# A gate vector's product moved from the attention of the first token half to the early feed-forward

## Chip, cores and metric

The kernel runs on one core of a Trainium2 chip. The metric is the device time of one execution in microseconds (us). The engines are TensorE (PE, with its weight loads shown as PEld), VectorE (DVE), ScalarE (ACT), GpSimd (POOL) and SyncE (SP, which here only issues transfers). They work side by side, each through its own list of instructions in a fixed order, and wait for each other by semaphores.

## What is computed

One layer of a decoder trunk for 1024 tokens of width 1024, in float32: a modulation by a conditioning vector, three mixers, an output projection, a feed-forward of width 4096. Cut to what matters here:

```
mod = silu(c) @ w_ada + b_ada
sh1, sc1, ga1, sh2, sc2, ga2 = split(mod, 6)          # vectors of 1024; their index v is 0..5
h = rms_norm(x, norm1_g) * (1 + sc1) + sh1
proj = h @ w_in
o_a = sliding window attention;  o_b = S5 state space;  o_c = sparse attention
mix = concat(rms_norm(o_a), rms_norm(o_b), rms_norm(o_c))
x = x + ga1 * (mix @ w_out)
h = rms_norm(x, norm2_g) * (1 + sc2) + sh2
x = x + ga2 * (square(relu(h @ w_ff1)) @ w_ff2)
```

The vector that the change concerns is ga2 (v = 5), the gate of the feed-forward. It is first needed when the feed-forward of the first token half is complete.

## The kernel before

Tokens are worked in eight tiles of 128 (n = 0 to 7), in two halves. The stages follow each other: modulation and first norm; input projection and S5; attention A and then C for tiles 0 to 3 (with their output projection, residual and second norm beside it); attention of tiles 4 to 7 mixed with the feed-forward of the first half; output projection of the second half; feed-forward of the second half, in which TensorE does almost nothing but 128x512 products. Each float32 product is made of three: every operand is split in a high part (a copy on ACT) and a low part (a subtraction on DVE or POOL).

The feed-forward of the first half can't begin before tile 3 has gone through all of its steps: the last attention unit, `finish_steps` (square, scaling by the norm's gain on POOL, high part on ACT, low part on DVE), the projection with `WO`, `residual`, and `norm2_steps`.

**A gate vector.** Each of the six vectors is made from eight slabs of `w_ada` (128 x 1024 float32, 512 KB each, one for each 128 outputs j). Vectors 2 to 5 are made by `ada2`, slab by slab: a transfer on SP's queue, eight ACT instructions that scale 128 columns each with one element of silu(c) (`prod` with `on_act`), a sum over 1024 columns on DVE, a product with a column of ones on PE, whose one column of output is evacuated by a small DVE addition. At the end of vectors 2 and 5 one transposition on PE, a copy on DVE and a transfer of 4 KB put the vector into `mod_d`, from where `load_row(5)` fetches it as a row for all partitions. The lines:

```
def ada2(v, pace):
    for j in range(KD):
        slab = page(1024)
        nc.sync.dma_start(out=slab, in_=I["ada"][v, j])
        yield pace
        a, z = page(128, "s"), tbank()[:, 0:1]
        prod(a, slab, True)
        PE.matmul(out=z, lhsT=a, rhs=ones[:, 0:1], start=True, stop=True)
```

**What sets the order.** Nothing is written out by hand. Steps are recorded in the order of a plan: each has a plan time, and generators such as `ada2` say after how much plan time their next step comes. `F_ADA` gives for each vector the plan time of its first slab and the pace between its steps. The recorded calls are then ordered by `arrange`: for each engine it takes the ready instruction that was recorded earliest, with fixed prices for each kind of instruction, PSUM banks and buffers. Plan times are numbers of that planner and no times of the chip.

**Buffers.** `page(1024)` takes one of 38 buffers with the tag b (4 KB in each partition). Slabs, their products, raw weights, and their high and low parts all share these; a transfer waits on SP until its buffer is free, and everything behind it on SP's queue waits too. PSUM: the small product of a slab takes its turn in the banks that the transpositions use (`tbank`), three during the attention of the first half, two beside the feed-forward.

Of the kernel before, what the change touches and what calls it, by code (L numbers as in the profile page):

```python
# [33 lines left out]
LAG = 2  # L34
BACC = dict(dynamic_dma_scratch_size=1024)
MOD_N = 2
F_ADA = {2: (40.0, 3.0), 4: (64.0, 5.0), 3: (110.0, 5.0), 5: (240.0, 5.0)}
F_LOAD, F_ROT, A_START = 0.635, 3.5, 0.0
A_DUR, A_LEAD, A_GAP = 6.0, 8.0, 2.0
P_START, P_TILE, C_START, C_CMP, C_LEAD0, C_CPACE = 2.38, 7.0, 0.0, 27.6, 5.0, 2.0  # L40
# [270 lines left out]
def trunk(ctx: ExitStack, tc: tile.TileContext, I, out):  # L311
# [85 lines left out]
    def spawn(t, gen, after=None):  # L397
        put(t, (gen, after))
# [924 lines left out]
# [9 lines that stand above are left out]
            b = VT[:, 16 + v * 8 + j:17 + v * 8 + j]  # L1332
            if v == 4:
                stt(mod_c[v][:, j:j + 1], z, 1.0, b, ALU.add, ALU.add)
            else:
                tt(mod_c[v][:, j:j + 1], z, b, ALU.add)
        if v == 4:
            tt(mod_c[v], mod_c[v], VT[:, 8:16], ALU.mult)
        if v in (2, 5):
            z, r = tbank()[0:8, 0:128], page(128)[0:8]  # L1340
            PE.transpose(z, mod_c[v], ident)
            V.tensor_copy(out=r, in_=z)
            nc.scalar.dma_start(out=mod_d[v // 3], in_=r)
        done.add(f"mod {v}")
# [5 lines left out]
    def front():  # L1350
        for v, (t0, pace) in F_ADA.items():
            spawn(t0, ada2(v, pace))
        spawn(now[0] + 40, load_group("aq", 2.0))
        yield from startup()
        t0 = now[0]
        spawn(t0, s5_taps(), "parameters")
        spawn(t0 + 0.5, paced(s5(), S_PACE), "parameters")
        spawn(t0 + F_ROT, paced(s5_rotation_table(), R_PACE))
        spawn(t0 + F_CA, s5_readout_table(), "rotation")
        names = NAMES  # L1360
        width = dict(WGROUPS)
        groups = dict(akv=group_akv, aq=group_aq, cq=group_cq, cmp=group_cmp, ck=group_ck, cv=group_cv)
        for i, name in enumerate(names):
            if name == A_AT:
                spawn(now[0], a_phase(), "KA")
                slow[0] = A_SLOW
            if i + 1 < len(names):
                dur = width[name] * 24 * 8 / 2400.0 * slow[0]
                spawn(now[0] + F_LOAD * dur, load_group(names[i + 1], dur * 0.1))
            yield from groups[name]()  # L1370
            if name == "cmp":
                spawn(now[0] + C_CMP, paced(compresses(), C_CPACE), "s5 taken")
        spawn(now[0] + P_START, early_ab())
        spawn(now[0], c_phase(), "compressed 1")
# [890 lines left out]
```

## Time and profile before

| what | value |
|---|---|
| three runs | 1403.05, 1407.94 and 3282.17 us; median 1407.94 us |
| profiled execution | 1406.35 us |
| its span, from the first to the last instruction | 1404.6 us |
| outside of the span | 1.75 us |
| TensorE's clock granted over the span, share of full | 0.962 |
| busy: PE, DVE, ACT, POOL | 1330.2, 973.0, 796.8, 652.9 us |

The page and the answers count an engine as busy while an instruction of it runs; matmuls are pipelined and their ends are modelled, so that a busy PE may still have slack. In a list of instructions in order of time, the bracket behind a row is the idle time of the engine just before it, and who ended it. Most program lines carry one line number (2201, where the recorded calls are played), so rows are told apart by tile names: b, u, s, q, k and r are buffer tags, pa and pb PSUM banks, small a collection of columns. Every slab product on ACT reads `b<-b,small 128x128`.

### The profile page before, as it was taken

What the parts mean: (1) busy time and instruction counts of PE and PEld (TensorE: products, weight loads), DVE (VectorE), ACT (ScalarE), POOL (GpSimd) and SP (SyncE); (2) the same over time, 40 slices, a digit from 0 to 9 for tenths busy, and PEclk for the clock granted to TensorE, in tenths of its full rate; (3) what the DMA queues carried; (4) which work ended last, traced back from release to release, by engine and by line L of the source; (5) the groups of instructions that cost most, each with busy time, mean ns of one, the idle gap of its engine ahead of it and who ended that gap; (6) DMA issues with size and microseconds to landing.
All of it is one profiled execution on the core that took longest, in us unless ns stands there. A gap on an engine that the chain in (4) does not pass through costs nothing.

```text
span 1404.6 us, 20524 instructions
## 1 busy us (share of the span) xinstructions
PE 1330.2 (95%) x7134; PEld 1142.1 (81%) x7134; DVE 973.0 (69%) x2005; ACT 796.8 (57%) x1816; POOL 652.9 (46%) x640
## 2 busy tenths in 40 slices
PE   5799799999899868999999999999999999999998
PEld 4689799999898647888888888888887888888886
DVE  7867658788688764556565566564559787888796
ACT  5368457777679766655556565553253545444450
POOL 2646756413656544546545546575564221222231
PEclk9979899999899877999999999999999999999999
DMA  9434434523224231222222232233556423233231
GB/s 360 151 106 134 153 101 135 196 81 106 66 73 147 94 134 37 96 68 72 75 68 88 75 98 68 99 111 109 168 175 241 164 77 102 94 107 118 64 102 60
DMA packets 59429, 160.55 MB, mean 114 GB/s; under 512 B 6431, under 2 KB 22333, under 8 KB 59325
## 3 DMA queue, kind: packets, MB, share of 16 engines
q1 hardware_dynamic: 51517, 145.33, 31.0%
q10 hardware_dynamic: 7808, 13.91, 2.7%
q8 instruction: 56, 0.92, 0.3%
q14 instruction: 48, 0.39, 0.1%
HBM read 140.07 MB, written 19.14 MB: 113 GB/s over the span
## 4 chain that ended last, share of the span: by engine, by line
PE 72%; DVE 5%; ACT 4%; issue 1%; DMA 0%; POOL 0%; ACTq 0%
PE pb L2201 41%; PE pa L2201 31%; ACT b L2201 3%; DVE b L2201 2%; ACT u L2201 1%; DVE pb L2201 1%; DVE k L2201 0%; DVE u L2201 0%; DMA cq_d<-s 0%; DVE small L2201 0%; DVE s L2201 0%; ACT s L2201 0%; ACT k L2201 0%; POOL s L2201 0%; ACTq L2201 0%
## 5 line engine op out<-in xcount | busy, mean ns | idle before, releaser
L2201 PE MATMUL pb<-b,b 128*128 128x512 f32 (+2 forms) x2478 | 591.9, 386 | 3.7 <-DVE b L2201 3.7
L2201 PEld LDWEIGHTS pb<-b,b 128*128 128x128 f32 (+1 forms) x2478 | 446.9, 190 | 87.3 <-DVE b L2201 5.1
L2201 POOL TENSOR_TENSOR b<-b,b 128x1024 fp32r<-128x1024 f32 (+6 forms) x140 | 317.7, 2276 | 319.2 <-ACT b L2201 211.5
L2201 PE MATMUL pa<-b,b 128*128 128x256 f32 (+2 forms) x1974 | 367.3, 336 | 10.8 <-DVE b L2201 6.0
L2201 PEld LDWEIGHTS pa<-b,b 128*128 128x128 f32 (+1 forms) x1974 | 302.4, 195 | 44.5 <-DVE b L2201 8.0
L2201 ACT ACTIVATE b<-b 128x1024 fp32r<-128x1024 f32 (+5 forms) x265 | 241.1, 926 | 114.1 <-DVE b L2201 44.4
L2201 DVE TENSOR_TENSOR b<-b,b 128x1024 fp32r<-128x1024 f32 (+4 forms) x181 | 203.2, 1153 | 18.2 <-ACT b L2201 11.2
L2201 PE MATMUL pa<-u,b 128*128 128x384 f32 (+2 forms) x836 | 208.1, 369 | 4.4 <-ACT u L2201 2.4
L2201 PEld LDWEIGHTS pa<-u,b 128*128 128x128 f32 x836 | 148.9, 208 | 15.6 <-ACT u L2201 7.9
L2201 DVE TENSOR_TENSOR b<-pa,b 128x512 f32<-128x512 f32 (+3 forms) x176 | 108.6, 626 | 69.7 <-PE pa L2201 66.1
L2201 ACT ACTIVATE u<-pa 128x384 fp32r<-128x384 f32 (+4 forms) x205 | 97.2, 479 | 93.5 <-PE pa L2201 91.0
L2201 DVE TENSOR_TENSOR u<-pa,u 128x384 fp32r<-128x384 f32 (+1 forms) x173 | 95.0, 553 | 63.0 <-ACT u L2201 59.9
L2201 DVE TENSOR_TENSOR b<-pb,b 128x512 f32<-128x512 f32 (+2 forms) x120 | 76.0, 647 | 53.0 <-PE pb L2201 51.0
L2201 POOL TENSOR_SCALAR b<-b,small 128x64 f32<-128x64 f32 (+8 forms) x118 | 78.1, 673 | 61.7 <-DVE small L2201 51.7
L2201 POOL TENSOR_SCALAR u<-u,small 128x256 f32<-128x256 f32 (+3 forms) x90 | 52.6, 595 | 115.2 <-DVE small L2201 78.7
L2201 PE MATMUL pa<-wide,b 128*128 128x128 f32 (+1 forms) x443 | 84.4, 303 | 14.5 <-DVE b L2201 10.2
L2201 ACT ACTIVATE b<-b,small 128x128 f32<-128x128 f32 x256 | 93.3, 529 | 1.8 <-DMA b<-in_ada_dram 0.9
L2201 PEld LDWEIGHTS pa<-wide,b 128*128 128x128 f32 (+1 forms) x443 | 59.4, 152 | 33.7 <-DVE b L2201 13.0
L2201 PE MATMUL pb<-k,u 128*128 128x320 f32 (+10 forms) x300 | 73.0, 352 | 8.6 <-ACT u L2201 5.8
L2201 ACT ACTIVATE b<-pb,small 128x64 f32<-128x64 f32 (+4 forms) x130 | 62.2, 493 | 30.1 <-DVE small L2201 24.5
L2201 POOL TENSOR_TENSOR b<-r,b 128x512 fp32r<-128x512 f32 x37 | 52.3, 1412 | 54.8 <-ACT b L2201 54.6
L2201 ACT ACTIVATE u<-pb,small 128x256 f32<-128x256 f32 (+6 forms) x126 | 59.7, 484 | 28.3 <-DVE small L2201 26.4
(150 smaller groups left out, 1511.1 us busy)
## 6 DMA issues: line engine op xcount, KB each, us to landing
b<-in_ff_dram SPq DMA_DIRECT2D x128, 512.0 KB, 3.9
b<-in_ada_dram SPq DMA_DIRECT2D x48, 512.0 KB, 5.2
b<-in_x_dram SPq DMA_DIRECT2D x16, 512.0 KB, 6.1
b<-in_wo_dram SPq DMA_DIRECT2D x16, 512.0 KB, 4.5
r<-in_w_in_dram SPq DMA_DIRECT2D x16, 256.0 KB, 2.7
b<-in_cw_dram SPq DMA_DIRECT2D x8, 512.0 KB, 4.5
x_d<-b ACTq DMA_DIRECT2D x8, 512.0 KB, 4.1
out_dram<-b SPq DMA_DIRECT2D x16, 256.0 KB, 3.0
```

The lines of the kernel that those rows point to most:

```text
L2201: method(*args, **kw)
```

## The change

One entry of the table changes. The first slab of vector 5 gets plan time 560 in place of 240, and the pace between its steps is 8 in place of 5.

```
-F_ADA = {2: (40.0, 3.0), 4: (64.0, 5.0), 3: (110.0, 5.0), 5: (240.0, 5.0)}
+F_ADA = {2: (40.0, 3.0), 4: (64.0, 5.0), 3: (110.0, 5.0), 5: (560.0, 8.0)}
```

What is computed stays the same. The order of all engines changes from the attention of the first half on, because `arrange` orders anew around the gap and around the new place.

**First place, ACT, the end of tile 3's attention.** Here s_717 (before) and s_707 (after) are the attention output of tile 3, s_769 and s_750 its squares, b_768 and b_749 its high part; b_773, b_779 are products of the last two slabs; small is fed by exponentials of tile 4's first unit (u_775, u_753). Before:

```order
L2201 ACTIVATE b_773<-b_766,small 128x128 x4
L2201 ACTIVATE b_779<-b_774,small 128x128 x2
L2201 ACTIVATE s_767<-pa_66 64x384
L2201 ACTIVATE small<-small 128x1
L2201 ACTIVATE u_770<-pa_65,small 128x384
L2201 ACTIVATE u_775,small<-pb_67,small 128x256 x2
L2201 ACTIVATE u_775,small<-pb_68,small 128x256
L2201 ACTIVATE s_769<-s_717 128x384
L2201 ACTIVATE small<-small 128x1 x2
L2201 ACTIVATE b_779<-b_774,small 128x128 x3
L2201 ACTIVATE b_768<-s_717 128x384
L2201 ACTIVATE b_779<-b_774,small 128x128 x3
```

And now, where b_766 is the high part of a feed-forward weight:

```order
L2201 ACTIVATE b_766<-b_765 128x1024
L2201 ACTIVATE s_748<-pa_66 64x384
L2201 ACTIVATE small<-small 128x1 x2
L2201 ACTIVATE u_753,small<-pb_67,small 128x256
L2201 ACTIVATE u_751<-pa_65,small 128x384
L2201 ACTIVATE s_750<-s_707 128x384
L2201 ACTIVATE u_753,small<-pb_67,small 128x256
L2201 ACTIVATE u_753,small<-pb_68,small 128x256
L2201 ACTIVATE small<-small 128x1
L2201 ACTIVATE b_749<-s_707 128x384
```

The slab products are gone from between the steps of tile 3, and a copy of a feed-forward weight has moved ahead of them.

**Second place, DVE and POOL, a few steps on.** On DVE, before, the sum of the last slab (s_778) stands between the masks of tile 4 (ISA) and the low part of tile 3 (b_768):

```order
L2201 ISA pb_67,small<-pb_67,u_465,small 128x256
L2201 ISA small 128x1
L2201 TENSOR_REDUCE s_778<-b_779 128x128
L2201 TENSOR_TENSOR b_768<-s_717,b_768 128x384
L2201 TENSOR_REDUCE small<-small 128x3
```

Now:

```order
L2201 ISA pb_67,small<-pb_67,u_465,small 128x256
L2201 ISA small 128x1
L2201 TENSOR_TENSOR b_749<-s_707,b_749 128x384
L2201 TENSOR_REDUCE small<-small 128x3
L2201 RECIPROCAL small<-small 128x3
```

On POOL, before, with b_789 the low part of the first feed-forward weight and s_717 as above:

```order
L2201 TENSOR_TENSOR s_717<-s_717,small 128x384
L2201 TENSOR_SCALAR u_775<-u_775,small 128x256
L2201 TENSOR_SCALAR small<-small 128x1
L2201 TENSOR_SCALAR u_775<-u_775,small 128x256
L2201 TENSOR_TENSOR small<-small 128x1
L2201 TENSOR_SCALAR u_775<-u_775,small 128x256
L2201 TENSOR_TENSOR b_789<-b_787,b_788 128x1024
```

Now, with b_764 and b_767 the low parts of the first two feed-forward weights:

```order
L2201 TENSOR_TENSOR b_764<-b_762,b_763 128x1024
L2201 TENSOR_TENSOR s_707<-s_707,small 128x384
L2201 TENSOR_TENSOR b_767<-b_765,b_766 128x1024
L2201 TENSOR_SCALAR small<-small 128x1
L2201 TENSOR_SCALAR u_753<-u_753,small 128x256
```

The sum has left DVE's list here; POOL's subtractions for the first two weights have moved around the scaling of tile 3, one of them directly behind it.

**Third place, SP and PE beside the feed-forward.** SP's queue at the loads of tile 7's queries (q from aq_d and cq_d), before:

```order
L2201 DMA q_1096<-aq_d 128x384
L2201 DMA b_1111<-in_ff_dram 128x1024
L2201 DMA q_1106<-cq_d 128x384
L2201 DMA b_1122<-in_ff_dram 128x1024
L2201 DMA q_1145<-cq_d 128x384
L2201 DMA b_1130<-in_ff_dram 128x1024
```

Now:

```order
L2201 DMA q_1071<-aq_d 128x384
L2201 DMA b_1082<-in_ada_dram 128x1024
L2201 DMA b_1087<-in_ff_dram 128x1024
L2201 DMA q_1081<-cq_d 128x384
L2201 DMA b_1096<-in_ada_dram 128x1024
L2201 DMA b_1101<-in_ff_dram 128x1024
L2201 DMA q_1133<-cq_d 128x384
L2201 DMA b_1109<-in_ada_dram 128x1024
L2201 DMA b_1112<-in_ff_dram 128x1024
L2201 DMA b_1120<-in_ada_dram 128x1024
```

All eight slabs stand in front of a feed-forward weight each. On PE the product of the first slab (pa_65<-ones) now stands inside a feed-forward product (pb_69), where no such row stood:

```order
L2201 MATMUL pb_69<-b_720,b_1061 128x512
L2201 MATMUL pb_69<-b_724,b_1061 128x512
L2201 MATMUL pb_69<-b_720,b_1062 128x512
L2201 MATMUL pa_65<-ones,s_1094 128x1
L2201 MATMUL pb_69<-b_721,b_1061 128x512
```

## Rows read from the trace of the kernel before

**Rows 1.** The page: busy tenths of PE in 40 equal slices; the chain's shares.

```profile
PE   5799799999899868999999999999999999999998
...
PE 72%; DVE 5%; ACT 4%; issue 1%; DMA 0%; POOL 0%; ACTq 0%
```

**Rows 2.** Busy us of each engine (instructions), clock and DMA, stretch by stretch.

```profile
core 0: us, PE busy (x) PEld busy (x) DVE busy (x) ACT busy (x) POOL busy (x), PEclk, DMA share, GB/s
416.00:433.00 17.00, 16.74 (x124) 15.38 (x123) 14.52 (x50) 14.66 (x43) 10.34 (x16) 1.00 0.40 130
433.00:448.00 15.00, 13.30 (x78) 11.36 (x77) 12.93 (x45) 13.93 (x44) 9.74 (x11) 0.89 0.57 203
448.00:463.00 15.00, 14.71 (x118) 14.18 (x117) 12.62 (x40) 11.14 (x37) 7.58 (x10) 1.00 0.26 78
463.00:473.00 10.00, 8.66 (x57) 7.12 (x57) 9.36 (x26) 7.20 (x21) 8.59 (x10) 1.00 0.48 157
473.00:483.00 10.00, 7.46 (x25) 3.83 (x23) 6.33 (x11) 9.27 (x25) 5.69 (x5) 0.66 0.29 107
483.00:507.00 24.00, 18.60 (x83) 13.45 (x82) 15.64 (x41) 23.46 (x73) 2.94 (x6) 0.78 0.42 139
507.00:536.00 29.00, 15.98 (x67) 11.98 (x68) 16.39 (x38) 14.16 (x36) 17.44 (x15) 0.62 0.30 105
...
840.00:870.00 30.00, 30.00 (x154) 25.30 (x153) 17.30 (x49) 17.95 (x43) 20.35 (x15) 1.00 0.23 69
```

**Rows 3.** Groups of ACT instructions from 410 to 510 us, shapes apart: the costliest.

```profile
L2201 ACT ACTIVATE b<-b,small 128x128 f32<-128x128 f32 x64 | 25.6, 532 | 0.1
```

**Rows 4.** ACT in order of time (start us, us), at the end of tile 3's attention.

```profile
498.26 2.03 ACT L2201 ACTIVATE b<-b,small 128x128 f32<-128x128 f32 x6
...
503.61 1.11 ACT L2201 ACTIVATE b<-b,small 128x128 f32<-128x128 f32 x3
504.50 0.54 ACT L2201 ACTIVATE b<-s 128x384 fp32r<-128x384 f32 x1
```

**Rows 5.** The chain that ended last, in order of time (start us, us, what).

```profile
416.98 2.60 ACT b L2201 x9
...
434.48 1.86 ACT b L2201 x6
...
448.27 2.29 ACT b L2201 x7
```

**Rows 6.** The same chain, a later stretch.

```profile
498.41 1.51 ACT b L2201 x5
```

**Rows 7.** POOL in order of time: tile 3's scaling, the first feed-forward weight's low part.

```profile
503.44 0.83 POOL L2201 TENSOR_TENSOR s<-s,small 128x384 f32<-128x384 f32 x1 [22.36 <-ACT s L2201]
...
507.95 2.34 POOL L2201 TENSOR_TENSOR b<-b,b 128x1024 fp32r<-128x1024 f32 x1 [1.18 <-ACT b L2201]
```

**Rows 8.** DVE in order of time: the last slab's sum, tile 3's low part.

```profile
506.86 1.21 DVE L2201 TENSOR_REDUCE s<-b 128x128 f32<-128x1024 f32 x1
507.99 2.72 DVE L2201 TENSOR_TENSOR b<-s,b 128x384 fp32r<-128x384 f32 x1
```

**Rows 9.** DVE instructions on s buffers, 410 to 511 us (ns min/median/max).

```profile
L2201 DVE TENSOR_REDUCE s<-b x8: 1210/1220/1223, 420.8 to 506.9; 128x128 f32<-128x1024 f32 x8
...
L2201 DVE TENSOR_TENSOR b<-s,b x3: 547/556/2720, 423.3 to 508.0; 128x384 fp32r<-128x384 f32 x3
```

**Rows 10.** PE in order of time: tile 3's projection begins.

```profile
510.77 4.34 PE L2201 MATMUL pa<-b,b 128*128 128x256 f32 x23 [4.10 <-DVE b L2201]
```

**Rows 11.** PE in order of time: slab products beside the input projection.

```profile
153.45 0.59 PE L2201 MATMUL pa<-ones,s 128*128 128x1 f32 x2 [4.73 <-DVE s L2201]
...
168.26 0.38 PE L2201 MATMUL pa<-ones,s 128*128 128x1 f32 x2 [1.96 <-DVE s L2201]
...
228.89 0.28 PE L2201 MATMUL pa<-ones,s 128*128 128x1 f32 x2
```

**Rows 12.** PE instructions on s buffers, 90 to 300 us: slab products.

```profile
L2201 PE MATMUL pa<-ones,s x44: 164/250/373, 96.9 to 278.5; 128*128 128x1 f32 x44
```

**Rows 13.** What PE's weight loads waited for, 540 to 900 us (us, times, longest).

```profile
PEld pb L2201 <- ACT b L2201: 0.9, 3, 0.3
...
PEld pa L2201 <- POOL b L2201: 0.6, 2, 0.3
```

**Rows 14.** SP in order of time: the load of tile 7's queries.

```profile
809.49 0.33 SPq L2201 DMA_DIRECT2D q<-aq_d  x1
```

## The prediction

> **What bounds the kernel now.** I read the page first: PE is busy nine tenths or more in nearly every slice from 16 on, each slice being 35.1 us, and PE has 72% of the chain that ended last; the weak slices after the first five are slice 10 and slices 13 to 15, the latter between 456 and 562 us [rows 1]. So a microsecond of PE's list costs a microsecond almost everywhere behind 562 us, and a microsecond of waiting saved ahead of it comes through to the end. Then I read the stretches [rows 2]. From 840 to 870 us PE is busy 30.00 of 30 us at full clock, with ACT at 17.95. From 473 to 507 us it is the other way round: ACT is busy 9.27 + 23.46 = 32.73 of 34 us, PE 7.46 + 18.60 = 26.06, at a granted clock of 0.66 and 0.78. From 507 to 536 no engine is near full; the steps of tile 3 follow one another there. So one stretch is bound by ACT, the next by a chain through all engines, and the rest by PE. The groups of ACT instructions say what fills ACT: the largest group between 410 and 510 us are the 64 slab products of vector 5 [rows 3].
>
> **What is removed.** The order shows that all 64 products, eight sums, eight small matmuls and eight loads leave this place, so the change does what it says. One product costs ACT not its 532 ns but its pitch: six in a row take 2.03 us, so (2.03 - 0.53) / 5 = 0.30 us [rows 4]; 64 of them are 19.2 us. They act in three places.
>
> Term 1, four slabs between 416 and 473 us. The chain runs through ACT in three pieces of 2.60, 1.86 and 2.29 us, nearly all slab products [rows 5], 6.8 us together. But PE is idle only 0.26 + 1.70 + 0.29 + 1.34 = 3.6 us in these 57 [rows 2], so PE would take over as the bound. If the clock of 0.89 from 433 to 448 went to full as well, 13.30 x 0.11 = 1.5 us more would go. Bounds 0 and 5.1; I take 3.5, PE's idle time.
>
> Term 2, four slabs from 473 to 507 us, 32 products; 26 stand ahead of 503.6 us and cost 26 x 0.30 = 7.8 us of an ACT without a gap. If PE bound instead, with its present 26.06 of 34 us, 7.9 us would go, so PE doesn't cut it further. The low end is the longest piece of slab products that the chain itself shows in this stretch, 1.5 us [rows 6]. Since ACT is at 96% here, I take a value near the high end: 6.5.
>
> Term 3, the way from tile 3's scaling to its projection. POOL's scaling ends at 503.44 + 0.83 = 504.27 us [rows 7]. Three products delay the high part on ACT to 504.50 us [rows 4]; the last sum holds DVE from 506.86 us, and the low part then runs from 507.99 to 510.71 us [rows 8], and PE stands idle for 4.10 us before the projection [rows 10]. That is 6.44 us from scaling to low part. Three products (0.9 us) and the sum (1.2 us) go. The low part took 2.72 us, two others of its shape 547 and 556 ns [rows 9]; it ran while POOL made a weight's low part from 507.95 to 510.29 us [rows 7], and ended 0.42 us after it. In the new order POOL has such a subtraction directly behind the scaling, so I let the low part lose to it again: 2.34 + 0.55 = 2.9 us in place of 6.44, a gain of 3.5. Bounds: 2.1 (products and sum alone) and 4.1 (PE's idle time there).
>
> The Trainium skill (SBUF — State Buffer, Who interferes with whom) says that a DVE operation with two inputs in SBUF and a GpSimd operation that reads SBUF exclude each other, and the first to start keeps the port to its end. The row agrees: 2.72 us beside a POOL row of 2.34. By that rule a second subtraction of POOL that starts ahead of the low part would cost another 2.34 us, and the time would be 1400; by the rows taken here it is 1398.
>
> Together 3.5 + 6.5 + 3.5 = 13.5 us.
>
> **What is added.** The slabs now begin behind the load of tile 7's queries, which stood at 809.49 us [rows 14]. ACT has room: 17.95 of 30 us, so even within 60 us the eight slabs' 19.2 us make it 35.9 + 19.2 = 55.1 of 60. DVE has 17.30 of 30 and gets 1.22 us per slab [rows 2, 9]. DMA is at 0.23 of its share there [rows 2]. On SP each slab stands in front of a feed-forward weight, and slab and product hold two of the 38 buffers; but PE's weight loads waited only 0.9 and 0.6 us for split weights in 360 us [rows 13], so I cost the later loads at nothing; what hides them is the weights' lead, and if that were used up, a wait of ACT's or POOL's splits would show at the first product of each unit.
>
> PE is full there, so its own instructions count: eight pairs and one transposition at no more than 0.28 us [rows 11], 9 x 0.28 = 2.5 us (low end nothing, where they fall into an existing gap). What they cost ahead of 536 us was covered by ACT's time.
>
> A wait is added too. PE works in order, and a slab's product waits for the sum. Behind it on PE stand feed-forward products, on which the whole end hangs. Between 90 and 300 us the same thing stood beside a busy PE: 44 records, so 22 slabs [rows 12], of which two made PE wait, 4.73 and 1.96 us [rows 11]. That is 6.69 / 22 = 0.30 us each, 2.4 us for eight. Bounds: nothing, and 8 x 4.73 = 37.8 us.
>
> **The sum.** -13.5 + 2.5 + 2.4 = -8.6 us. Durations are from the profiled execution, 1406.35 us (span 1404.6 and 1.75 outside): 1397.8, so **1398 us**. The median of the three runs shown is 1407.94, 1.6 above that execution.
>
> **Rivals.** (a) The gain is eaten: tile 3's chain of hand-overs sets the pace even without slab products. Only the low ends go, 0 + 1.5 + 2.1 = 3.6 us, against 4.9 added: 1408 us. For it: 483 to 536 us has an idle PE also where ACT is idle (14.16 of 29 from 507). Against it: ACT at 23.46 of 24 us.
>
> (b) More is gained. With the high ends 5.1 + 7.8 + 4.1 = 17.0 and no wait of PE for the sums, the change gives 14.5 us. TensorE's granted clock falls to its lower level of 1.2 GHz for part of the stretches with idle PE: 0.62 of 2.4 GHz from 507 to 536 us [rows 2]. If a denser list kept it at the upper level there, 15.98 x 0.38 = 6.1 us of PE's work would go, about half of it on the chain: 3 us more. 1389 us. For it: the clock is 1.00 in every full stretch. Against it: PE's idle time from 517 on belongs to residual and norm of tile 3, which the change doesn't touch.
> The Trainium skill (TensorE: Matmul & The Clock Gate, What's actually happening) says that the halved clock is the default and that activity releases it; the rows agree, and by that rule alone the result would lie at this rival's side.
>
> (c) Slower: PE waits for the sums beside the feed-forward. The place is the eight small products; with two transposition banks and the in-order list each could cost the mean of the two waits, 3.35 us: -13.5 + 2.5 + 26.8 = +15.8, 1422 us. It decides from (13.5 - 2.5) / 8 = 1.4 us per slab on. For it: 4.73 us did happen. Against it: 20 of 22 slabs cost no such wait, and the products now stand among long feed-forward runs.
>
> **Chances.** Forecast 0.48 (its own range 1391 to 1404), (a) 0.24, (b) 0.20, (c) 0.08. The range 1386 to 1410 takes in the forecast, most of (a) with 2 us of scatter as the runs show it, and (b) with 3; it leaves out (c) and the tails, under 2 in 10. Two per cent is 28 us (about what a measurement of this kernel can tell from no change): under 1378 us only if (b) is surpassed by far, 0.04; over 1434 us only if every slab cost the worst wait (-13.5 + 2.5 + 37.8 gives 1433) and the gain were smaller too, 0.02; within 2%, 0.94.
>
> **What would show it.** Term 1: PE's idle time between 416 and the end of tile 2's attention falls to about nothing. Term 2: ACT shows gaps in the stretch where norm and attention of tiles 0 to 3 meet, and tile 3's scaling comes about 10 us earlier than 503.4. Term 3: the idle time before tile 3's projection falls from 4.10 to about 1 us. The first long run of feed-forward products starts about 13 us earlier, and the lead shrinks to 8 or 9 us by 900 us. Rows `pa<-ones,s` behind 800 us with brackets of more than a microsecond would speak for (c); a start of the feed-forward less than 5 us earlier, for (a). I would be wrong altogether if the new order put something else ahead of tile 3's steps, or if feed-forward weights came late.

## The result, and the profile after

The changed kernel takes 1389.8 us (median of four runs, 1384.09 to 1392.59), the kernel before 1406.76 us beside it, a median that counts one execution of 3282.17 us; without that one it is 1405.58 us, 15.8 us above the changed kernel, and the ratio is 0.9883, with an interval of 0.9837 to 0.9929. The profiled execution is one of 1392.59 us, with a span of 1390.8 against 1404.6 us: 13.8 us less. The forecast was 1398 us, 8.6 us less. Direction, order of size and place were right; the text below shows that not all of the terms were.

The page of the changed kernel, its lines that answer to [rows 1]; a slice is now 34.8 us:

```profile
PE   5799799999899869999999999999999999999998
...
PE 73%; DVE 4%; ACT 2%; issue 1%; POOL 1%; DMA 0%; ACTq 0%; DVEq 0%; POOLq 0%
```

ACT's share of the chain falls from 4% to 2%. The stretches of the changed kernel, with the columns and limits of [rows 2]:

```profile
416.00:433.00 17.00, 17.00 (x127) 15.99 (x126) 14.20 (x49) 11.86 (x33) 12.29 (x16) 1.00 0.40 124
433.00:448.00 15.00, 13.95 (x94) 12.10 (x93) 13.40 (x50) 12.58 (x40) 9.79 (x14) 1.00 0.41 146
448.00:463.00 15.00, 15.00 (x119) 14.41 (x118) 11.93 (x43) 7.96 (x26) 8.57 (x9) 1.00 0.04 7
463.00:473.00 10.00, 7.13 (x36) 4.71 (x35) 8.05 (x18) 7.89 (x19) 7.61 (x10) 0.85 0.55 202
473.00:483.00 10.00, 8.12 (x34) 5.63 (x33) 5.68 (x11) 8.60 (x24) 2.91 (x4) 0.64 0.30 107
483.00:507.00 24.00, 18.44 (x99) 14.61 (x98) 14.06 (x37) 15.90 (x46) 9.68 (x12) 0.86 0.19 60
507.00:536.00 29.00, 22.72 (x95) 17.39 (x94) 16.15 (x45) 20.95 (x52) 20.59 (x16) 0.76 0.30 105
840.00:870.00 30.00, 30.00 (x159) 25.45 (x158) 21.03 (x49) 25.92 (x70) 17.08 (x12) 1.00 0.37 120
```

From 483 to 507 us ACT falls from 23.46 to 15.90 of 24 us, and still PE is busy only 18.44, at a clock of 0.86: with ACT's load gone the stretch is not full on any engine. From 840 to 870 us PE stays full with ACT at 25.92 of 30.

The steps of tile 3, in the changed kernel. POOL in order of time, answering [rows 7]:

```profile
496.36 0.83 POOL L2201 TENSOR_TENSOR s<-s,small 128x384 f32<-128x384 f32 x1 [4.44 <-ACT s L2201]
497.14 2.37 POOL L2201 TENSOR_TENSOR b<-b,b 128x1024 fp32r<-128x1024 f32 x1
```

DVE, answering [rows 8]:

```profile
499.31 0.63 DVE L2201 TENSOR_TENSOR b<-s,b 128x384 fp32r<-128x384 f32 x1
```

PE, answering [rows 10]; this is the first of 32 such rows of tile 3's projection:

```profile
499.99 0.58 PE L2201 MATMUL pa<-b,b 128*128 128x256 f32 x1 [0.68 <-DVE b L2201]
```

The scaling comes 7.1 us earlier (503.44 to 496.36), the end of the low part 10.8 us (510.71 to 499.94), the first 128x512 product of the feed-forward 16.0 us (536.15 to 520.17). That product on PE, before and then now:

```profile
536.15 0.78 PE L2201 MATMUL pb<-b,b 128*128 128x512 f32 x1
```

```profile
520.17 0.78 PE L2201 MATMUL pb<-b,b 128*128 128x512 f32 x1
```

From there the lead shrinks a little, to 13.8 us at the end.

And the new slab products on PE, by tile, between 800 and 900 us (ns shortest/median/longest, first and last start):

```profile
L2201 PE MATMUL pa<-ones,s x16: 164/250/271, 818.2 to 879.2; 128*128 128x1 f32 x16
```

None of the 16 records (eight pairs, as in [rows 12]) has an idle PE before it. Rival (c) did not happen.

**A common measure.** Executions of these kernels differ by up to 8 us before the first slab of vector 5 is touched (more on that below). So I count each trace from one row that all kernels have, an exponential on ACT that starts at 357.75 us before and at 357.72 us after, and look at the stretch from 58.25 us behind it (416 us before) to the third relu of the feed-forward (563.7 us before, 547.8 after). Its rows, first of the kernel before:

```profile
416.00:563.70 147.70, 123.16 (x672) 100.03 (x671) 99.27 (x280) 111.10 (x318) 73.83 (x78) 0.84 0.32 108
```

and after:

```profile
416.00:547.80 131.80, 114.15 (x656) 94.97 (x655) 88.78 (x264) 92.49 (x254) 73.64 (x78) 0.88 0.27 93
```

The stretch is 15.9 us shorter. PE's idle time falls from 24.5 to 17.7 us, its busy time by 9.0 us. By the forecast's own term some 2.5 us of these 9.0 are the nine instructions that left; the rest falls as the clock rises. The granted clock has two levels, so a mean of 0.84 means the lower one for 2 x 0.16 x 147.7 = 47 us, and 0.88 for 2 x 0.12 x 131.8 = 32 us (an estimate from the two rows).

### The profile page after: what moved, and what is told of

Read it like the earlier page. It is cut to its first block, busy times and chain, and to the rows that moved or that the text cites. A ratio compares the mean times of both kernels' runs of the same rounds, so it can differ in the third digit from the quotient of the medians.

```text
span 1390.8 us, 20525 instructions
## 1 busy us (share of the span) xinstructions
PE 1324.6 (95%) x7134; PEld 1140.6 (82%) x7134; DVE 971.5 (70%) x2005; ACT 797.5 (57%) x1816; POOL 652.8 (47%) x640
## 4 chain that ended last, share of the span: by engine, by line
PE 73%; DVE 4%; ACT 2%; issue 1%; POOL 1%; DMA 0%; ACTq 0%; DVEq 0%; POOLq 0%
PE pb L2201 41%; PE pa L2201 32%; DVE b L2201 2%; ACT b L2201 1%; ACT u L2201 1%; DVE pb L2201 1%; DVE k L2201 1%; DVE u L2201 0%; POOL b L2201 0%; DVE s L2201 0%; DMA cq_d<-s 0%; DVE small L2201 0%; POOL u L2201 0%; ACT k L2201 0%; POOL s L2201 0%
## 5 line engine op out<-in xcount | busy, mean ns | idle before, releaser
L2201 PE MATMUL pa<-u,b 128*128 128x384 f32 (+2 forms) x836 | 205.1, 367 | 7.0 <-DVE u L2201 3.9
```

The costliest lines, as they stand in the source:

```text
L2201: method(*args, **kw)
```

## Experiments

Twelve kernels, each in five to twelve timed runs beside the kernel before, and each with a trace. All in one table: the ratio to before with its interval, and from the trace the stretch just defined, PE's idle time in it, and four places of tile 3, moved by the difference of the common row, so that they read on the clock of the kernel before. Scaling is the start of tile 3's scaling on POOL, the residual is written at the end of its addition on DVE, and the feed-forward begins with the first 128x512 product on PE.

| kernel | ratio | stretch, us | PE idle | scaling | low part ends | residual written | feed-forward begins |
|---|---|---|---|---|---|---|---|
| before | 1 | 147.7 | 24.5 | 503.4 | 510.7 | 526.5 | 536.2 |
| after | 0.988 [0.984, 0.993] | 131.8 | 17.7 | 496.4 | 500.0 | 512.3 | 520.2 |
| e1_none | 0.989 [0.987, 0.991] | 131.0 | 17.4 | 495.5 | 499.1 | 511.4 | 519.4 |
| e5_double | 0.991 [0.989, 0.993] | 130.5 | 17.3 | 495.2 | 498.7 | 511.0 | 518.9 |
| p400 | 0.991 [0.990, 0.993] | 131.4 | 17.5 | 495.8 | 499.4 | 511.8 | 519.7 |
| e8_dve_gate | 0.990 [0.989, 0.992] | 135.2 | 18.9 | 497.1 | 500.7 | 510.1 | 523.4 |
| e3_first_early | 0.993 [0.990, 0.995] | 137.4 | 17.6 | 497.3 | 501.4 | 514.5 | 525.6 |
| e4_second_early | 0.994 [0.992, 0.996] | 138.7 | 20.7 | 497.2 | 501.5 | 514.7 | 526.4 |
| e2_noprod | 0.990 [0.988, 0.991] | 135.5 | 16.6 | 495.1 | 497.7 | 509.7 | 522.2 |
| e6_prods_only | 0.991 [0.990, 0.993] | 134.6 | 17.1 | 498.4 | 501.1 | 510.4 | 523.3 |
| f1_all | 0.994 [0.991, 0.996] | 138.6 | 20.5 | 498.0 | 502.1 | 518.3 | 528.0 |
| f2_prods | 0.999 [0.997, 1.001] | 144.3 | 22.4 | 499.8 | 507.7 | 524.0 | 533.7 |
| f3_sums | 0.997 [0.994, 0.999] | 143.3 | 23.5 | 502.4 | 506.3 | 522.1 | 531.8 |
| q242 | 0.996 [0.994, 0.998] | 140.3 | 18.5 | 501.7 | 504.5 | 516.5 | 528.3 |

After, e1_none, e5_double and p400 have one and the same order up to the feed-forward; their stretches of 130.5 to 131.8 us say how well this measure repeats.

### The price beside the feed-forward

e1_none, in `ada2`:

```
-        for j in range(KD):
+        if v == 5:
+            V.tensor_copy(out=mod_c[v], in_=VT[:, 56:64])
+            yield pace
+        for j in range(KD if v != 5 else 0):
```

> The eight slabs of vector 5 (loads, products, sums, small matmuls) are left out altogether; the gate is then the bias alone, so this part of the computation is missing. Everything ahead of the feed-forward stands as in the changed kernel. Theory A (beside the feed-forward the slabs cost only TensorE's own eight instructions and one transposition, 0.25 us each): 2 us under the changed kernel, about 1388 on a chip where before takes 1406.8, and the first 128x512 product of the feed-forward starts at 520 us, as in the changed kernel. Rival B (the slabs delay weights through SP's queue, the buffers or the splits as well): 5 us or more under it.

e5_double, in `ada2`, behind the loop:

```
+        if v == 5:
+            for j in range(KD):
+                ...
+                prod(a, slab, True)
+                PE.matmul(out=z, lhsT=a, rhs=ones[:, 0:1], start=True, stop=True)
+                tt(mod_c[v][:, j:j + 1], z, VT[:, 16 + v * 8 + j:17 + v * 8 + j], ALU.add)
```

> As the changed kernel, with the eight slabs of vector 5 loaded, multiplied and summed a second time right behind the first, so sixteen slabs beside the feed-forward of the first half. Theory A (only TensorE's own instructions cost): 8 x 0.25 = 2 us over the changed kernel, and no small product of a slab makes TensorE wait. Rival B (weights, buffers or ACT's lead are used up): 5 us or more over it, with waits of TensorE for ACT or POOL at the start of feed-forward units.

The way from the third relu to the 33rd, through the whole feed-forward of the first half and into that of the second, takes 777.41 us before, 778.27 without any slab (e1_none), 779.84 with eight (after), 781.67 with sixteen (e5_double). So eight slabs cost 1.6 to 2.4 us. That is the size of TensorE's own time in theory A, and the second eight cost 1.8 us, no more than the first. The medians, 1388.6 and 1389.7 us, can't tell these apart.

p400 (the table's entry is `5: (400.0, 8.0)`):

> As the changed kernel with plan time 400 in place of 560, so that the slabs stand earlier beside the feed-forward, while attention of tiles 5 and 6 still runs beside it. Theory A (any place with a full TensorE and room on ACT has the same price of TensorE's own instructions): within 2 us of the changed kernel. Rival B (near the attention the slabs' products delay exponentials as they did in the first half): 4 us or more over the changed kernel, with TensorE waiting for ACT beside the slabs.

779.88 us for the same way, and the same stretch ahead of it: this second place within the full part costs the same. Theory A held. The median is 12.5 us under the kernel before beside it (1391.37 and 1403.83 us), for the same work and the same order up to the feed-forward as in the changed kernel; with the 15.8 us of the first section, the change is worth 12 to 16 us.

### Which half of the slabs

e3_first_early and e4_second_early give four slabs to a second generator; here the first:

```
-            spawn(t0, ada2(v, pace))
+            spawn(t0, ada2(v, pace, range(4, 8) if v == 5 else range(KD)))
+        spawn(240.0, ada2(5, 5.0, range(0, 4)))
```

> Slabs 0 to 3 at the place of before (plan time 240, pace 5), slabs 4 to 7 at the new place. Theory A (the gain adds up by place: 5.5 us for the slabs between 416 and 473 us, 11 us for those from 473 on, each by ACT's time and the hand-overs of tile 3): the gain of the second part alone, 11 less 1 for four slabs beside the feed-forward, so about 10 us under before, 1396 to 1397; tile 3's scaling on POOL 1.5 us earlier than before, tile 3's projection about 5 us earlier. Rival B (ACT's backlog is what counts, wherever it was made): half of the gain, 8 us under before. Rival C (the new order as a whole was lucky): no more than 3 us under before.

> The reverse: slabs 0 to 3 at the new place, slabs 4 to 7 at the plan time that they had before (260). Theory A: the gain of the first part alone, 5.5 less 1, so 4 to 5 us under before, about 1402; tile 0's write of its residual at 461 us as in the changed kernel, and tile 3's projection still behind a stall of several us. Rival B (backlog): 8 us under before. Rival C: no more than 3 us under before, and in no place earlier.

Moving the last four slabs alone shortens the stretch by 10.3 us, as theory A said; moving the first four alone by 9.0 us, twice what it said. Together they would make 19.3, but all eight gave 15.9 to 16.7. In both kernels tile 3's scaling comes 6 us earlier, although in e4_second_early 26 of the 32 products of four slabs still stand ahead of it, as many as before. This does not fit a load on ACT that is taken away place by place. Rival B, a backlog on ACT wherever it was made, said 8 us for each; the medians are 10.6 and 8.2 us under before. Against it stands f2_prods below: there all products go and the order stays, and the stretch is only 3.4 us shorter.

### Which part of a slab's work

Theory A was now that ACT's products hold the stretch up. e2_noprod, at the place of before:

```
-            prod(a, slab, True)
+            if v == 5:
+                V.tensor_reduce(out=a, in_=slab.rearrange("p (c k) -> p c k", k=KD), axis=AX.X, op=ALU.add)
+            else:
+                prod(a, slab, True)
```

> Vector 5 at the place of before (plan time 240, pace 5), with its loads, sums, small products and evacuations, but without the 64 products on ACT: the sum on DVE reads the slab itself, so the gate is wrong, as the scaling by silu(c) is missing. Theory A (ACT's 19.2 us are what held up the stretch): nearly all of the early gain comes, the way from 416 us of before to the third relu of the feed-forward is 13 us shorter or more (147.7 us before, 131.8 in the changed kernel), 12 to 14 us under before in all. Rival B (the gain came from the slabs' transfers, buffers, sums and TensorE's small products): 5 us or less under before.

e6_prods_only, there too:

```
+            if v == 5:
+                m = page(1024).rearrange("p (c k) -> p k c", k=KD)
+                for k in range(KD):
+                    A.activation(out=m[:, k], in_=slab..., func=AF.Copy, scale=cT[:, k:k + 1])
+                V.tensor_copy(out=mod_c[v][:, j:j + 1], in_=VT[:, 56 + j:57 + j])
+                continue
```

> The reverse: vector 5 at the place of before, with its loads and its 64 products on ACT, but without sums and small products; the gate is then the bias alone. Theory A: ACT is as full as before, so only the last sum ahead of tile 3's low part (1.2 us) and TensorE's own instructions (2.5 us where TensorE is the bound) go: 2 to 4 us under before, the same way 143 us or longer. Rival B: 10 us or more under before.

Without the products 12.2 us of the stretch go, nearly the 13 of theory A. Without the sums, with every product on ACT, 13.1 us go, which breaks it. Here is the stretch of e6_prods_only:

```profile
413.10:547.70 134.60, 117.46 (x654) 95.71 (x653) 89.32 (x264) 110.07 (x317) 77.10 (x78) 0.87 0.35 118
```

ACT is busy 110.07 us in it, nearly as much as in the kernel before (111.10), in 13.1 us less. So a full ACT was not what made the stretch long. Either the sums were, or it was something that all of these kernels share: `arrange` makes a new order in each of them.

### Load or order

The next three kernels keep the order of before and take the work out behind it, so that no other instruction moves; q242 does the reverse, all of the work and a new order. At the end of `trunk` (`kind` marks vector 5's calls; DROP is load, prod, sum and mm for f1_all, prod for f2_prods, sum and mm for f3_sums):

```
         for i in order:
             _, _, method, args, kw = calls[i]
-            method(*args, **kw)
+            k, slab = kind.get(i, (None, None))
+            if k in DROP:
+                continue
+            if k == "sum" and "prod" in DROP:
+                kw = dict(kw, in_=slab.rearrange("p (c k) -> p c k", k=KD))
+            ...
+            method(*args, **kw)
```

> The kernel before with its order kept on every engine, from which the loads, products, sums and small products of vector 5 are taken out behind the ordering (a copy of the bias stands in place of each evacuation; the gate is then the bias alone). So the load goes and no other instruction moves. Theory A (load: what the slabs' work itself costs the stretch): the way from 416 us to the third relu is as short as without the slabs in the new order, 131 to 133 us in place of 147.7, 15 us or more under before. Theory C (order: the new order around tile 3 gives a good part by itself): 138 to 142 us, 6 to 10 us under before.

> The kernel before with its order kept, without the 64 products of vector 5 on ACT (the sums read the slabs, so the scaling by silu(c) is missing). Theory A (ACT's load): 8 to 12 us under before, the same way 136 to 140 us. Theory C (order): no more than 6 us under before, as the same work left out with a new order gave 12.2 us in that way.

> The kernel before with its order kept, without the sums and the small products of vector 5; loads and the 64 products stay where they were (the gate is then the bias alone). Theory A (load): 13.1 us of that way go here too, as they did where the order was made anew without the sums. Theory C (order): ACT is as full as before and tile 3's chain keeps its neighbours, so only the last sum ahead of tile 3's low part and TensorE's own instructions go, 2 to 5 us, and the rest of the 13.1 us belonged to the order.

q242, a change of the kernel before:

```
-5: (240.0, 5.0)}
+5: (242.0, 5.0)}
```

> The kernel before with plan time 242 in place of 240 for vector 5: all of its work stays beside the attention of the first half, only the order of the engines' lists is made anew; on ACT the three exponentials of tile 4's first unit now stand behind the squares of tile 3's attention output and no longer ahead of them. Theory A (load): within 3 us of before, the way from 416 us to the third relu 145 us or longer. Theory C (order): 5 to 12 us under before, 136 to 143 us.

The stretches of f1_all, f2_prods, f3_sums and q242, in this order:

```profile
411.20:549.90 138.70, 118.21 (x656) 96.40 (x655) 88.78 (x272) 92.60 (x254) 73.83 (x78) 0.88 0.26 89
```

```profile
410.40:554.80 144.40, 121.97 (x667) 99.49 (x666) 98.23 (x279) 92.29 (x252) 72.95 (x77) 0.85 0.32 110
```

```profile
411.90:555.30 143.40, 119.92 (x663) 97.13 (x663) 89.52 (x275) 111.43 (x320) 74.91 (x80) 0.87 0.33 111
```

```profile
413.00:553.40 140.40, 121.94 (x674) 98.97 (x673) 96.37 (x281) 111.78 (x318) 75.63 (x78) 0.87 0.34 114
```

With the order kept, taking out all of the slabs' work gives 9.1 us; a new order with all of the work gives 7.4 us. Theory C is right on f1_all, f2_prods, f3_sums and q242 alike. Four pairs of kernels do the same work in the order of before and in a new one: before and q242 differ by 7.4 us, f1_all and e1_none by 7.6, f2_prods and e2_noprod by 8.8, f3_sums and e6_prods_only by 8.7. So order is nearly half of what the change gains, with the slabs' work and without it. As all four new orders give a shorter stretch than the old one, it looks as if the order of before was a bad one; four orders do not prove it.

9.1 + 7.4 = 16.5 comes near what the change did (15.9) and e1_none (16.7), but that is in part chance: q242's order is not that of the changed kernel, and both numbers hold one place, tile 3's low part, as shown below. The changed kernel's own order is the step from f1_all to e1_none: 9.1 + 7.6 = 16.7. The ratios stand in the same row of sizes: 0.999, 0.997, 0.996, 0.994 for f2_prods, f3_sums, q242 and f1_all.

Of the load's 9.1 us the products, 19.2 us of ACT, give 3.4, and the sums and small products give 4.4; the other 1.3 us, loads or all of it together, were not parted. Most of the 4.4 are one place. (In these three kernels the calls are played from line 2218.) DVE in f2_prods, where the last sum is still there:

```profile
498.31 1.22 DVE L2218 TENSOR_REDUCE s<-b 128x128 f32<-128x1024 f32 x1
499.44 2.73 DVE L2218 TENSOR_TENSOR b<-s,b 128x384 fp32r<-128x384 f32 x1
```

and in f3_sums, where it is not:

```profile
501.72 0.56 DVE L2218 TENSOR_TENSOR b<-s,b 128x384 fp32r<-128x384 f32 x1
```

POOL, first in f2_prods, then in f3_sums:

```profile
499.41 2.35 POOL L2218 TENSOR_TENSOR b<-b,b 128x1024 fp32r<-128x1024 f32 x1 [1.18 <-ACT b L2218]
```

```profile
502.82 2.38 POOL L2218 TENSOR_TENSOR b<-b,b 128x1024 fp32r<-128x1024 f32 x1 [1.18 <-ACT b L2218]
```

In f2_prods POOL began the subtraction of a feed-forward weight at 499.41 us, 0.03 us ahead of the low part, which then took 2.73 us. Without the sum the low part is first, 1.1 us ahead of POOL's subtraction at 502.82 us, and takes 0.56. So the sum cost 1.2 us, and its delay let POOL in first, for 2.2 us more.

Most of what the changed kernel's order gives is behind the low part. From its end to the writing of the residual it takes 15.8 us before, 16.2, 16.3 and 15.8 in f1_all, f2_prods and f3_sums, and 9.4 to 13.2 in every kernel with a new order. POOL before (the first of two is the product with the gate row, 2.35 us long), then DVE:

```profile
517.62 4.67 POOL L2201 TENSOR_TENSOR b<-b,b 128x1024 f32<-128x1024 f32 x2 [0.43 <-DVE b L2201]
```

```profile
519.94 0.62 DVE L2201 SCALAR_TENSOR_TENSOR u<-pa,small,u 128x384 fp32r<-128x384 f32 x1 [1.30 <-ACT u L2201]
521.85 0.47 DVE L2201 CUSTOM_DVE_ANT_0 pb<-pb,b 128x288 f32<-128x288 f32 x1 [1.29 <-PE pb L2201]
...
522.70 0.58 DVE L2201 CUSTOM_DVE_ANT_0 pb<-pb,b,small 128x352 f32<-128x352 f32 x1
...
523.39 3.11 DVE L2201 TENSOR_TENSOR b<-b,b 128x1024 f32<-128x1024 f32 x1
```

The gate product was ready at 519.97 us, but the addition that waits for it stands on DVE behind the masks of tile 4's scores, and those waited for PE; it began 3.4 us later. In q242 the product ended at 511.6 us, and DVE ran:

```profile
511.82 0.47 DVE L2201 CUSTOM_DVE_ANT_0 pb<-pb,b 128x288 f32<-128x288 f32 x1
...
512.20 1.36 DVE L2201 TENSOR_TENSOR b<-b,b 128x1024 f32<-128x1024 f32 x1
```

In the changed kernel the addition follows the product at once. POOL, the product and a weight's low part behind it, and DVE:

```profile
506.50 4.69 POOL L2201 TENSOR_TENSOR b<-b,b 128x1024 f32<-128x1024 f32 x2 [3.14 <-DVE b L2201]
```

```profile
508.90 3.36 DVE L2201 TENSOR_TENSOR b<-b,b 128x1024 f32<-128x1024 f32 x1 [0.62 <-POOL b L2201]
```

So in the changed kernel 3.4 us of waiting ahead of the addition are gone, by its place in DVE's list; the collision with POOL stays. The table gives the rest of its order, from f1_all to e1_none: 2.5 us ahead of the scaling, 0.5 from there to the end of the low part, 3.9 from there to the residual, 1.7 from there to the feed-forward; of these 8.6 us, 1.0 is lost again behind. The last two ways go by the order alone: from the residual to the feed-forward it takes 9.7 us in all four kernels with the order of before, whatever work is left out, and 7.9 us in all four with the order of the changed kernel. What made the 2.5 and the 1.7 us was not taken apart.

In q242 the parts are others: 1.8 us ahead of the scaling, 4.4 at the low part, which the last sum no longer precedes (it ends 2.8 us behind the start of the scaling and not 7.3), and 3.8 up to the residual, where the wait falls from 3.4 to 0.6 us and the addition from 3.11 to 1.36; 2.2 us of it are lost between residual and feed-forward, and 0.4 behind. The 4.4 us at the low part are the place that the load's 9.1 us hold too, with 3.2 (f1_all).

### An attempt to go on

The 3.36 us above are a collision with POOL again. e8_dve_gate:

```
-        tt(y[n], y[n], rows_of[2], ALU.mult, G)
+        tt(y[n], y[n], rows_of[2], ALU.mult, V if n == 3 else G)
```

> As the changed kernel, but the multiplication of tile 3's projection with the gate row, 2.38 us on POOL, is put on DVE, where adding the residual stands right behind it. Theory A (behind tile 3's projection the path to the feed-forward runs POOL 2.38, DVE 3.36, and the long DVE row is a collision with POOL's weight split): the path gets 2 to 3 us shorter, the feed-forward starts that much earlier, 2 us under the changed kernel. Rival B (DVE then waits for POOL's split at the port, once for the multiplication and once for the addition): no change or 1 to 2 us over it.

DVE in e8_dve_gate, the gate product and the addition:

```profile
499.94 1.23 DVE L2201 TENSOR_TENSOR b<-b,b 128x1024 f32<-128x1024 f32 x1
...
501.55 1.21 DVE L2201 TENSOR_TENSOR b<-b,b 128x1024 f32<-128x1024 f32 x1
```

POOL and then DVE in it, some steps on, at the second norm of tile 3 (the norm's factor, a weight's low part; masks of tile 4's next unit, the scaling by that factor):

```profile
505.35 0.55 POOL L2201 TENSOR_TENSOR small<-small 128x1 f32<-128x1 f32 x1
...
509.42 2.35 POOL L2201 TENSOR_TENSOR b<-b,b 128x1024 fp32r<-128x1024 f32 x1
```

```profile
508.47 0.47 DVE L2201 CUSTOM_DVE_ANT_0 pb<-pb,b 128x288 f32<-128x288 f32 x1 [0.24 <-PE pb L2201]
...
509.03 0.59 DVE L2201 CUSTOM_DVE_ANT_0 pb<-pb,b,small 128x352 f32<-128x352 f32 x1
...
509.72 2.59 DVE L2201 TENSOR_SCALAR b<-b,small 128x1024 f32<-128x1024 f32 x1
```

The same scaling in the changed kernel:

```profile
515.20 0.74 DVE L2201 TENSOR_SCALAR b<-b,small 128x1024 f32<-128x1024 f32 x1
```

At the residual the collision is gone, and it is written 2.2 us earlier, as theory A said. But the order was made anew, and now the norm's scaling, whose factor was ready at 505.90 us, stands on DVE behind masks of tile 4, 3.8 us late, and meets POOL there: 2.59 us in place of 0.74. The feed-forward begins 3.2 us later than in the changed kernel, and the stretch is 3.4 us longer. The ratio, 0.990, tells no difference to the changed kernel. It is once more the place of one step in DVE's list that costs the time. No version that beats the changed kernel was found.

The Trainium skill (SBUF — State Buffer, Who interferes with whom) says that a DVE operation with two SBUF inputs and a GpSimd operation that reads SBUF lock each other out, and that the one issued first goes first. The rows here agree: 0.56 or 2.73 us for the same low part, 1.21 or 3.36 us for the same addition, and in f2_prods 0.03 us decided. The scaling of 0.74 or 2.59 us has only one large input, so the collision reaches further here than that sentence; the same section lists tensor_scalar apart, among the operations that can contend too.

## Why the prediction was right, and where it was not

**Terms 1 and 2, ACT's products.** Forecast 3.5 + 6.5 = 10.0 us, measured 3.4 (f2_prods). Tile 0's residual is written 2.4 us earlier in that kernel (466.64 to 464.28), which is term 1; to tile 3's scaling the lead grows to 3.6 us, so term 2 is 1.2 us and not 6.5. With loads, sums and small products out as well, the scaling comes 5.4 us earlier (f1_all). The step that failed is "since ACT is at 96% here, I take a value near the high end". A busy share is no bound by itself: without the products ACT is busy 18.8 us less (111.10 to 92.29) in a stretch that is only 3.4 us shorter, so nearly all of their time turns into waiting. The low end of that term, 1.5 us from the chain [rows 6], was the better reading.

**Term 3, the last sum and the low part.** Forecast 3.5 us; with the order kept the way from the start of the scaling to the end of the low part falls from 7.3 to 4.1 us (f1_all), 3.2 us less, and to 3.6 us in the changed kernel. Right in size. But the forecast let the low part collide with POOL again, for 2.9 us from the end of the scaling to its own; in the changed kernel that way takes 2.75 us without it: POOL's subtraction was nearly over, and the low part took 0.63 us.

**What was not forecast.** 7.6 us from the order itself (f1_all to e1_none). The prediction took the new order as the old one without the slabs, and named a change of it only as a danger. The order showed that two of tile 4's three exponentials had moved behind the squares of tile 3; no term came of it.

**What was added.** TensorE's own instructions: forecast 2.5 us, measured 1.6 to 2.4. TensorE's waits for the sums: forecast 2.4 us, measured none. The price per wait came from a place where PE ran products of 128x384 and less; among 128x512 products no sum came late. That their length is the reason was not tested.

**The sum.** With the measured terms: 9.1 by load and 7.6 by order, less 2.4, make 14.3 us; the spans differ by 13.8. The forecast had 13.5 - 4.9 = 8.6. Ahead of the feed-forward a term of 10.0 that was 3.4 stood for 7.6 us that were left out, which is luck. The difference to the result, 5.2 us, is 2.5 of the 4.9 us of cost, which did not come, and 2.4 ahead of the feed-forward (15.9 in place of 13.5), but for 0.3. The medians are 17.0 us apart, and 15.8 without the execution of 3282.17 us, 2 us more than the spans; traces scatter by more than that in their first 290 us, below.

**The rivals.** The result lies at the number of rival (b), 1389, and two of its conditions came true: TensorE's clock rose, from 0.62 to 0.76 between 507 and 536 us and from 0.84 to 0.88 over the stretch, and no sum made PE wait. Its high ends for ACT's work are refuted by f2_prods. What stood against it, that the change doesn't touch residual and norm of tile 3, was wrong: the new order shortened just these. Rival (a), that tile 3's hand-overs set the pace even without slab products, was nearer to what happened than the forecast's terms 1 and 2; but its price for that, 3.6 us in all, left out that a new order changes these hand-overs. Rival (c) is refuted by the rows on PE.

**The marks.** PE's idle time to the end of tile 2's attention did fall, from 2.25 to 1.05 us between 416 and 463; over all of the 57 us of term 1 it is 3.9 us, against 3.6 before. ACT does show gaps. Tile 3's scaling came 7 and not 10 us earlier, the first wrong sign of term 2. The idle time before tile 3's projection fell to 0.68 us. The feed-forward began 16 and not 13 us earlier, and the lead shrank to 13.8 and not to 8 or 9.

## What to carry to other kernels

Where a change makes the order of all engines anew, price the new order as a term of its own: walk the one chain that sets the end through the new lists, and look at what stands ahead of each of its steps on each engine. An engine that is busy 96% of a stretch need not be its bound; take the length of its pieces in the chain before its busy time. To part load from order, take the work out behind the ordering, and beside it change the order with the work kept.

## What was not expected of the hardware

The kernels have the same instructions up to 290 us, and yet one and the same product on PE starts there at 289.17 us before and 281.12 us in e3_first_early. The windows from 36 us up to it, first before, then e3_first_early:

```profile
36.00:289.17 253.17, 231.03 (x1519) 217.59 (x1519) 182.41 (x320) 152.09 (x389) 141.16 (x193) 0.91 0.42 137
```

```profile
36.00:281.12 245.12, 225.70 (x1519) 213.00 (x1518) 182.71 (x320) 151.91 (x389) 143.09 (x193) 0.94 0.43 141
```

The same number of products, the same busy time on ACT and DVE, and 8.0 us between them: 5.3 us more of PE's busy time at a clock of 0.91 against 0.94, and 2.7 us more of waiting. What decides it from one execution to the next stays open. It is as large as half of the change's effect, so that single times tell less here than the traces counted from a common row.
